# Low parts of raw operands by an adding DMA in the paired down projection of a two-layer encoder

## The chip, the cores and the metric

The kernel runs on one core of a Trainium2 chip. The metric is the time of one launch in microseconds of the device: the median of the runs before is 3236.0 us (three runs, 3235.75 to 3237.17).

## What is computed

Two post-norm layers of an encoder trunk over 1024 tokens of width 1024, float32 in and out. A layer has an input projection to four kinds of mixers, an output projection with a layer norm, a gated MLP with 2816 inner features and a layer norm, and a gated embedding with a layer norm. The change lies in the last product of the MLP:

```
f = silu(dwconv(h @ w_gate)) * (h @ w_up)      # [1024 tokens, 2816 features]
h = layer_norm(ALPHA * h + f @ w_down)         # w_down [2816, 1024]
```

## The kernel before

**Products in two parts.** TensorE multiplies tiles of a reduced float32 form (`F32R`). To keep the precision of float32, an operand is split in a high part, the value rounded to that form, and a low part, the rest. `split` (L92 to L94) does it in two operations: ScalarE copies the source to the high part (L84), and VectorE or GpSimd subtracts the high part from the source (L87). A product then is the sum of three: high with high, high with low, low with high (`p3`). The profile gives the helper's line for all such operations, L84 for ScalarE's and L87 for two-tile operations on VectorE or GpSimd; what they work on is told by the names of the tiles.

**The paired down projection** (`down_paired`, L1511 to L1621). Of the 22 tiles of 128 inner features, the first 20 go through it, in 5 rounds (`ch`) of 4 tiles. In a round the tokens fall in two halves, the outputs in two halves and the feature tiles in two pairs, so that the round is a product of 2 x 2 blocks, a11 to a22 (features) times b11 to b22 (weights). It is computed by Winograd's scheme with 7 products in place of 8. Each product has two operands, and each operand two tiles of 128 x 512 (the two feature tiles of a pair), to be split. Some operands are blocks as they come from memory (raw): a11 and b11 in product 1, a12 and b21 in product 2, b22 in product 3, a22 in product 4. The others are sums and differences of blocks (`comb`), made in place.

**Sources and tiles.** Features come from `fd` in DRAM, written by the stage before, into tiles named `fr`; weights come from `ffn_w_down` into tiles named `wr` (in round 0 two of the four into `wraw`). All are loaded by SyncE's queue in the order 0, 2, 1, 3. The split parts stand in tiles named `part`, one tile per operand with both parts; eight tiles share the tag, so four products' operands are alive at a time, and ScalarE's first pass of a new operand waits until TensorE is done with the one four products back. `part(srcs, eng)` (L1522) splits an operand; features' low parts are made on GpSimd, weights' on VectorE.

**The order of a round** is that of `operands` (L1555 to L1569): products 1, 2, 5, 7, 6, 3, 4, with the combinations between them, some on VectorE and some on GpSimd. Products are issued two operands behind (L1614 to L1621). Each product is four quarters of 128 tokens, six matmuls each (L1582). Product 1 of all rounds adds up in PSUM (`first`, tile `pp`). The other quarters are evicted: in round 0 products 5, 6, 7 by ScalarE to `E`, the others by VectorE to `H` with a factor (L90); in later rounds all by VectorE, added to `E` or `H` (L87). In the last round `merge` joins E and H.

**What sets the order on the engines.** Every engine works through its own queue in order. The queues are not written by hand: a planner that simulates the kernel with its own costs goes through the program, places instructions of neighbouring steps among one another, and puts in the waits. So the queues' order need not be that of the text, and where a step's operations change, the order around it can change too.

**Adding DMAs.** The kernel before has none. GpSimd's queue issues only DMAs that load the transform's constants and masks in the mixers (L397, L212 to L216); in the stage of the change all DMAs are SyncE's.

Of the kernel before, what the change touches and what calls it, by code (L numbers as in the profile page):

```python
# [28 lines left out]
# columns of the packed per-layer parameters  # L29
# [4 lines left out]
# feature tiles of the input projection  # L34
# [8 lines left out]
def interleave(*flows):  # L43
    """Emits flows, each (generator, number of its steps), in step with one another."""
    live = [[g, 0, n] for g, n in flows]
    while live:
        f = min(live, key=lambda f: f[1] / f[2])
        try:
            next(f[0])
            f[1] += 1  # L50
        except StopIteration:
            live.remove(f)


def stagger(items):
    """Emits the stages of items so that each item is one stage behind the one before it."""
# [18 lines left out]
class Trunk:  # L75
# [16 lines left out]
    def split(self, hi, lo, src, eng=None):  # L92
        self.act(hi, src)
        self.tt(lo, src, r(hi), ALU.subtract, eng)  # L94

# [50 lines left out]
    def to_x_after(self, x, H, t0, t1, ins, pair=False):  # L146
        """Transposes token tiles t0 to t1, once the products up to ins have freed the tiles that the
        result goes to."""
# [11 lines left out]
    def layer_norm(self, h, gb, eps=None, first=None):  # L160
        """The statistics; returns two functions that normalise h in place, one after the other."""
# [16 lines left out]
        def affine(c=512):  # L178
            """The first c columns, scaled already, on GpSimd, the others on VectorE."""
# [74 lines left out]
    def embed(self):  # L254
        """Normalises the input; the second half of the tokens only when the function that is returned runs."""
# [43 lines left out]
    def sin_of(self, fp, out, pre):  # L299
        """out = sin(pre) with the argument brought to [-pi, pi]."""  # L300
# [99 lines left out]
    def bruun(self, pool, zm, zp, C):  # L400
        """Residues of a polynomial of 1024 coefficients (8 blocks of 128 rows, C columns each)
        modulo the eight factors of x^2048 - 1 of degree 256; zm and zp are its residues modulo
        x^1024 - 1 and x^1024 + 1."""
# [36 lines left out]
    def conv_fft(self, l, n, pool, z, feature_major, out):  # L440
        """Circular convolution of z (token-major, 8 x 256) with filter n, and the skip term that the
        filter holds; the result is token-major [128, 8 * 256] or feature-major [128, 2, 8 * 128]."""
# [112 lines left out]
    def in_half(self, x, w, ps, hf):  # L555
        c0 = hf * 512
        if not isinstance(w, tuple):
            # the products of the high and the low parts of the weights, in separate rows
# [5 lines left out]
    def in_proj(self, l, x, tile_i):  # L564
        """One tile of 128 features, [128, 1024] in PSUM, in two steps."""
# [7 lines left out]
    def conv3(self, out, ps, cw):  # L573
        """Centred 3-tap convolution along the free dim with bias: cw columns w0, w1, w2, b."""
# [4 lines left out]
    def mixers(self, l, x, mu, late, st0):  # L579
# [9 lines left out]
        def scalars(su, ps):  # L589
            """Rotary key and dt, token-major."""  # L590
# [24 lines left out]
        def latent(pr, ti, k, rs, last, n):  # L615
            """A latent of attention with its gain, to DRAM; the sums of its squares go to rs."""
# [140 lines left out]
    def token_sums(self, sq):  # L757
        """Sums over features of the tiles sq [128 features, 512 tokens], as [128, 4] with tokens on partitions."""
# [5 lines left out]
    def squares(self, ss, g, hf, y, sq):  # L764
        """For the sums of squares of group g for 512 tokens, whose features are y, tokens on partitions:
        returns the function that finishes them on the tensor engine."""
# [6 lines left out]
    def ssd_scalars(self, l, mu, dtr):  # L773
# [5 lines left out]
        # softplus(x) = max(x, 0) + log1p(exp(-|x|)), the log by its series in e / (2 + e)  # L779
# [32 lines left out]
        # log(dt) - acs  # L812
# [6 lines left out]
    def ssd(self, l, ss, scal, xbc, zd, yd):  # L819
# [17 lines left out]
        def jv(a, c, g, n):  # L837
            """Columns (direction, head) of a group, broadcast over n."""
            return a[:, c, :].rearrange("p (d h) -> p d h", d=2)[:, :, 2 * g:2 * g + 2].unsqueeze(3).to_broadcast([128, 2, 2, n])

        def states(c, g):
            # token-major x and B, chunk states, forward scan
# [92 lines left out]
    def hl_products(self, out, terms):  # L935
        """Products of a [K, 2, 64] (hi and lo) with b, hi and lo: the sum of out[0:64] and out[64:128]."""
# [228 lines left out]
    def out_weights(self, l, g, pool):  # L1165
        """The rows of the output projection of a group, times the gains of its norm."""
# [12 lines left out]
    def out_proj(self, l, st, yd, ss, w, ahead):  # L1179
        nc, t = self.nc, self.t  # L1180
        hp = self.pool(st, f"hp{l}", 8, side=RIGHT)
        with ExitStack() as so:
# [17 lines left out]
            def scales(g):  # L1200
                # the residual branch is left unscaled: H holds the sum over ALPHA
# [73 lines left out]
    def blocks(self, todo, j):  # L1275
        """Transposes blocks of 128 tokens and 512 features, each (from, PSUM, (hi, lo)), to the
        128 tokens j of the operands."""
# [77 lines left out]
    def gate_up(self, l, H, hp, x, fd):  # L1355
        """The inner features of the MLP, to fd. Up and gate are the two rows of a product of blocks
        A (features x halves of D) and B (halves of D x halves of the tokens), by Winograd's scheme
        of seven products."""
        nc, t, pp = self.nc, self.t, self.pp[l]
        add, sub = ALU.add, ALU.subtract  # L1360
        with ExitStack() as st:
# [22 lines left out]
            def first(w1, w2, eng=None):  # L1384
                """The products of the first row of A and the first column of B."""
# [57 lines left out]
            for j in range(4):  # L1443
# [3 lines left out]
                # T1 = B12 - B11, T3 = B22 - B12, T2 = B22 - T1, and B21 - T2 for T4  # L1447
# [63 lines left out]
    def down_paired(self, l, fd, hmid, H, dp, ft):  # L1511
        """ALPHA times H plus the products of the first PAIRED inner features, by Winograd's scheme of seven
# [291 lines left out]
```

## Time and profile before

| | |
|---|---|
| median of three runs | 3236.0 us (3235.75 to 3237.17) |
| profiled execution, first to last instruction (its span) | 3236.6 us |
| mean granted TensorE clock, share of full speed | 0.965 |
| TensorE busy | 2976.9 us (92%) |
| VectorE busy | 2451.0 us (76%) |
| ScalarE busy | 1292.0 us (40%) |
| GpSimd busy | 1821.3 us (56%) |
| matmuls of the paired products (L1582), both layers | 1680 |

Only the span of the profiled execution is known, no time of its own beside it; it lies within the times of the runs. PE is TensorE, PEld its weight loads, DVE VectorE, ACT ScalarE, POOL GpSimd, SPq and POOLq the queues of DMA issues of SyncE and GpSimd. An instruction's row has its start and duration in us, engine, line, operation, the tile written and the tiles read, shapes, a count where several alike stand together, and in brackets the idle time of the engine before it with what ended it. Matmuls overlap, so a matmul's duration is longer than the distance to the next.

### The profile page before, as it was taken

The numbers are of one execution on the slowest core, as the hardware profiler recorded it, in microseconds if no ns is written. First come the engines' busy times: TensorE is split into PE (matmuls) and PEld (weight loads), VectorE is DVE, ScalarE is ACT, GpSimd is POOL, SyncE is SP. The second block draws the span as 40 slices with busy tenths as digits, with TensorE's granted clock in tenths as the row PEclk, the third lists the DMA queues.
The fourth block names the chain that finished last, engine by engine and source line by source line (L and its number), as shares of the span: only waits on it lengthen the run. The fifth ranks groups of instructions, "written<-read, shape, count | busy, mean of one in ns | idle before, by whom it ended". The sixth has DMA issues, their size and how long they took to land.

```text
span 3236.6 us, 40462 instructions
## 1 busy us (share of the span) xinstructions
PE 2976.9 (92%) x14316; PEld 2429.1 (75%) x14316; DVE 2451.0 (76%) x3711; ACT 1292.0 (40%) x2278; POOL 1821.3 (56%) x1371
## 2 busy tenths in 40 slices
PE   6999989998999999999989998899989999989996
PEld 4887866877777777777868877778777777767685
DVE  7678776878765557999777786778786555689986
ACT  4332365743333334333343323667333333343341
POOL 5455533527656556886435454345177555578855
PEclk9999998999999999999999998999999999999998
DMA  5566523022222225313335755130222222343232
GB/s 178 156 200 204 192 75 130 16 83 85 85 79 78 78 79 198 123 47 115 126 100 172 225 192 165 53 121 25 97 85 79 79 78 78 114 163 107 74 135 92
DMA packets 140468, 368.98 MB, mean 114 GB/s; under 512 B 15139, under 2 KB 42023, under 8 KB 140009
## 3 DMA queue, kind: packets, MB, share of 16 engines
q1 hardware_dynamic: 126008, 315.72, 28.8%
q0 software_dynamic: 14256, 50.67, 5.2%
q8 instruction: 114, 1.87, 0.2%
q14 instruction: 90, 0.73, 0.1%
HBM read 278.77 MB, written 87.56 MB: 113 GB/s over the span
## 4 chain that ended last, share of the span: by engine, by line
PE 39%; DVE 21%; POOL 16%; issue 10%; DMA 10%; ACT 4%; SPq 0%; POOLq 0%; DVEq 0%; ACTq 0%
PE ps L99 18%; PE pp L99 13%; POOL w L87 5%; DMA wraw<-in_ffn_w_gate_dram 4%; POOL wraw L87 4%; DVE part L87 3%; POOL u L87 2%; DVE fr L87 2%; POOL H L87 2%; PE ps L942 2%; DVE H L90 2%; DVE s L87 1%; POOL part L87 1%; DVE H L87 1%; DMA wraw<-in_ffn_w_up_dram 1%
## 5 line engine op out<-in xcount | busy, mean ns | idle before, releaser
L99 PE MATMUL ps<-x,w 128*128 128x512 f32 x2112 | 508.2, 394 | 11.3 <-ACT v L84 6.1
L99 PEld LDWEIGHTS ps<-x,w 128*128 128x128 f32 x2112 | 400.1, 190 | 99.1 <-ACT v L84 7.0
L99 PE MATMUL pp<-x,wh 128*128 128x512 f32 x1344 | 427.9, 397 | 1.8 <-ACT wh L84 1.8
L99 PE MATMUL ps<-xq,w 128*128 128x512 f32 x1584 | 391.1, 397 | 29.7 <-DVE u L87 24.3
L1582 PE MATMUL ps<-part 128*128 128x512 f32 x1440 | 351.2, 399 | 33.8 <-DVE H L87 10.8
L99 PEld LDWEIGHTS ps<-xq,w 128*128 128x128 f32 x1584 | 292.9, 188 | 117.2 <-DVE u L87 50.7
L1582 PEld LDWEIGHTS ps<-part 128*128 128x128 f32 x1440 | 270.9, 191 | 110.5 <-DVE H L87 20.3
L99 PEld LDWEIGHTS pp<-x,wh 128*128 128x128 f32 x1344 | 254.9, 192 | 54.3 <-ACT wh L84 2.0
L87 POOL TENSOR_TENSOR w<-wraw,w 128x512 fp32r<-128x512 f32 x164 | 217.5, 1345 | 116.0 <-ACT w L84 116.0
L99 PE MATMUL pp<-x,wl 128*128 128x512 f32 x672 | 266.5, 397 | 3.8 <-POOL wl L87 3.8
L84 ACT ACTIVATE w<-wraw 128x512 fp32r<-128x512 f32 x264 | 151.8, 622 | 268.0 <-DMA wraw<-in_ffn_w_up_dram 218.6
L87 POOL TENSOR_TENSOR wl<-wraw,wh 128x1024 fp32r<-128x1024 f32 (+2 forms) x61 | 152.8, 2507 | 182.7 <-ACT wh L84 124.2
L87 POOL TENSOR_TENSOR part<-fr,part 128x512 fp32r<-128x512 f32 x120 | 192.4, 1628 | 47.2 <-ACT part L84 42.2
L87 DVE TENSOR_TENSOR s<-wraw 128x512 f32<-128x512 f32 x44 | 55.4, 1259 | 202.2 <-DMA wraw<-in_ffn_w_gate_dram 199.8
L99 PE MATMUL ps<-wo,yn 128*128 128x512 f32 x768 | 189.7, 405 | 5.4 <-DVE H L90 3.0
L1039 POOL TENSOR_TENSOR P<-P,smr 128x1024 f32<-128x1024 f32 x64 | 121.1, 1893 | 112.2 <-DVE smr L1038 103.3
L99 PEld LDWEIGHTS ps<-wo,yn 128*128 128x128 f32 x768 | 147.1, 195 | 39.4 <-DVE H L90 4.8
L90 DVE SCALAR_TENSOR_TENSOR g<-g,pp 128x1023 f32<-128x1023 f32 x88 | 126.6, 1439 | 57.7 <-ACT g L84 57.7
L87 POOL TENSOR_TENSOR u<-u,g 128x512 f32<-128x512 f32 x44 | 78.7, 1788 | 152.5 <-ACT g L84 152.3
L87 DVE TENSOR_TENSOR part<-wr,part 128x512 fp32r<-128x512 f32 x124 | 158.2, 1299 | 4.8 <-ACT part L84 4.8
L99 PE MATMUL ps<-wh,x 128*128 128x512 f32 x512 | 158.8, 391 | 0.0
L99 PEld LDWEIGHTS pp<-x,wl 128*128 128x128 f32 x672 | 128.5, 191 | 30.5 <-POOL wl L87 4.7
(381 smaller groups left out, 7038.7 us busy)
## 6 DMA issues: line engine op xcount, KB each, us to landing
c_fwd<-in_c_fwd_dram POOLq DMA_DIRECT2D x64, 512.0 KB, 5.1
wraw<-in_ffn_w_up_dram SPq DMA_DIRECT2D x50, 512.0 KB, 3.5
wraw<-in_ffn_w_gate_dram SPq DMA_DIRECT2D x44, 512.0 KB, 4.5
f<-u SPq DMA_DIRECT2D x88, 256.0 KB, 2.0
wraw<-in_w_in_dram SPq DMA_DIRECT2D x42, 512.0 KB, 4.1
fr<-f SPq DMA_DIRECT2D x40, 512.0 KB, 4.5
wr<-in_ffn_w_down_dram SPq DMA_DIRECT2D x36, 512.0 KB, 6.4
c_inv<-in_c_inv_dram POOLq DMA_DIRECT2D x32, 512.0 KB, 5.0
```

The costliest lines, as they stand in the source:

```text
L84: self.nc.scalar.activation(out, in_, func, **kw)
L87: (eng or self.nc.vector).tensor_tensor(out, a, b, op=op)
L90: return self.nc.vector.scalar_tensor_tensor(out, a, s, b, op0=op0, op1=op1)
L99: ins = self.nc.tensor.matmul(out, a, b, start=i == 0, stop=i == n - 1)
L942: ins = self.nc.tensor.matmul(out[0:64] if j else out, v[:, 0, :] if j else v.rearrange("p i d -> p (i d)"), terms[i][1 + j], start=k == 0 ...
L1039: nc.gpsimd.tensor_tensor(P, P, sm.to_broadcast([128, T]), op=ALU.mult)
L1582: nc.tensor.matmul(ps, u, v, start=k == 0 and (p != 1 or ch == 0), stop=k == 5 and (p != 1 or ch == last))
```

## The change

The low parts of the raw operands are no longer subtracted by VectorE or GpSimd. ScalarE writes the high part as before, and then, from the same source, its negative into the place of the low part, rounded to the same form. A DMA issued by GpSimd's queue then reads the same block once more from DRAM (`fd` or `ffn_w_down`) and adds it to what stands there, which leaves source minus high part. In rounds 1 to 4 this is done for all six raw operands; in round 0 the two of product 1 are split as before, so four are changed. The operands made by combinations are split as before. The rest of the diff removes comments and docstrings only.

```diff
+    def split_added(self, hi, lo, src, far):
+        self.act(hi, src)
+        self.act(lo, src, scale=-1.0)
+        self.nc.gpsimd.dma_start(lo, far, accum_op=ALU.add)
...
-        def part(srcs, eng):
+        def part(srcs, eng, far=None):
             hl = self.xp.tile([128, 2, 2, 512], F32R, name="part", tag="X")
             for i, v in enumerate(srcs):
-                self.split(hl[:, i, 0], hl[:, i, 1], v, eng)
+                if far is None:
+                    self.split(hl[:, i, 0], hl[:, i, 1], v, eng)
+                else:
+                    self.split_added(hl[:, i, 0], hl[:, i, 1], v, far[i])
             return hl
...
-            F, W = {}, {}
+            F, W, fF, fW = {}, {}, {}, {}
             for k in (0, 2, 1, 3):
                 f = 4 * ch + k
+                fF[k], fW[k] = fd[f], t["ffn_w_down"][l, f * 128:(f + 1) * 128, :]
...
+            p11, p12, _, p22 = ([fF[2 * i + k][:, h] for i in range(2)] for h in (h0, h1) for k in range(2))
+            q11, q21, _, q22 = ([fW[2 * i + k][:, h] for i in range(2)] for h in (h0, h1) for k in range(2))
...
-            def operand(p, a, b):
-                return p, part(a, nc.gpsimd), part(b, nc.vector)
+            def operand(p, a, b, fa=None, fb=None):
+                return p, part(a, nc.gpsimd, fa), part(b, nc.vector, fb)
 
-            yield operand(1, a11, b11)
-            yield operand(2, a12, b21)
+            yield operand(1, a11, b11, p11 if ch else None, q11 if ch else None)
+            yield operand(2, a12, b21, p12, q21)
...
-            yield operand(3, a12, b22)
+            yield operand(3, a12, b22, None, q22)
             comb(b21, b11, b21, sub, nc.gpsimd)
-            yield operand(4, a22, b21)
+            yield operand(4, a22, b21, p22)
```

## Rows read from the trace of the kernel before

**Rows 1.** The page's head: span, and busy us of each engine.
```profile
span 3236.6 us, 40462 instructions
...
PE 2976.9 (92%) x14316; PEld 2429.1 (75%) x14316; DVE 2451.0 (76%) x3711; ACT 1292.0 (40%) x2278; POOL 1821.3 (56%) x1371
```

**Rows 2.** Stretches: length, busy us (instructions) per engine, clock, DMA share, GB/s.
```profile
1260.00:1280.00 20.00, 15.12 (x55) 10.85 (x53) 20.00 (x18) 10.26 (x19) 17.74 (x11) 0.91 0.32 93
1300.00:1320.00 20.00, 14.23 (x54) 10.53 (x53) 20.00 (x18) 7.25 (x14) 20.00 (x13) 0.91 0.03 8
1340.00:1360.00 20.00, 19.72 (x86) 15.69 (x85) 19.32 (x21) 8.12 (x16) 18.68 (x13) 1.00 0.04 6
2900.00:2920.00 20.00, 14.94 (x57) 11.17 (x56) 20.00 (x22) 7.89 (x15) 18.30 (x12) 0.91 0.31 106
```

**Rows 3.** Line 1582: what ended its engine's idle time (us, times).
```profile
  DVE H L87: 31.0, 37
  DVE part L87: 22.7, 14
  DVE E L87: 13.4, 21
  ACT E L84: 13.3, 12
  DVE H L90: 12.1, 9
```

**Rows 4.** Timeline of TensorE at both ends of the stage, both layers.
```profile
1251.77 5.60 PE L1582 MATMUL pp<-part 128*128 128x512 f32 x24
1257.21 3.11 PE L1582 MATMUL ps<-part 128*128 128x512 f32 x13
...
1467.50 4.82 PE L1582 MATMUL ps<-part 128*128 128x512 f32 x18 [0.54 <-DVE H L87]
...
2845.68 5.60 PE L1582 MATMUL pp<-part 128*128 128x512 f32 x24
...
3060.28 4.83 PE L1582 MATMUL ps<-part 128*128 128x512 f32 x18 [0.59 <-DVE H L87]
```

**Rows 5.** The splits: the page's groups, then ScalarE's copies with min/median/max in ns.
```profile
L87 POOL TENSOR_TENSOR part<-fr,part 128x512 fp32r<-128x512 f32 x120 | 192.4, 1628 | 47.2 <-ACT part L84 42.2
L87 DVE TENSOR_TENSOR part<-wr,part 128x512 fp32r<-128x512 f32 x124 | 158.2, 1299 | 4.8 <-ACT part L84 4.8
...
L84 ACT ACTIVATE part<-fr x120: 613/625/637, 1235.3 to 3041.0; 128x512 fp32r<-128x512 f32 x120
```

**Rows 6.** Timeline of VectorE and GpSimd, side by side and VectorE alone.
```profile
1300.52 1.74 POOL L87 TENSOR_TENSOR part<-tg,part 128x512 fp32r<-128x512 f32 x1
1301.03 1.78 DVE L87 TENSOR_TENSOR tg<-fr 128x512 f32<-128x512 f32 x1
...
1334.52 0.68 DVE L87 TENSOR_TENSOR fr<-tg,fr 128x512 f32<-128x512 f32 x1
```

**Rows 7.** Timeline of GpSimd: two DMA issues, one after the other.
```profile
222.88 1.10 POOL L397 DMA_DIRECT2D c_fwd<-in_c_fwd_dram  x2
```

**Rows 8.** DMA: GpSimd's queue, a 256 KB store, landing of the 512 KB loads from GpSimd.
```profile
q0 software_dynamic: 14256, 50.67, 5.2%
...
f<-u SPq DMA_DIRECT2D x88, 256.0 KB, 2.0
...
DMA to landing us min/median/max: 3.7/5.1/8.1
```

**Rows 9.** Timeline of round 0 in layer 0, ahead of its second product.
```profile
1253.62 3.98 POOL L87 TENSOR_TENSOR wraw<-wr,wraw 128x512 f32<-128x512 f32 x2
...
1255.27 1.19 DVE L87 TENSOR_TENSOR part<-wr,part 128x512 fp32r<-128x512 f32 x1
```

**Rows 10.** Timeline of the start of round 2 in layer 0.
```profile
1330.29 1.16 ACT L84 ACTIVATE part<-fr 128x512 fp32r<-128x512 f32 x2 [3.23 <-issue]
...
1335.48 0.62 PE L1582 MATMUL pp<-part 128*128 128x512 f32 x2
```

## The prediction

> **What bounds the kernel now.** The page comes first: TensorE is busy for 92% of 3236.6 us and VectorE for 76% [rows 1], so over the whole span TensorE seems to be the limit. That is an average, and the change touches one stage of each layer, the paired down projection, so the second view is the table of stretches there [rows 2]. In a good stretch (1340 to 1360) TensorE starts 86 matmuls in 20 us. In 1260 to 1280 and 1300 to 1320 it starts 55 and 54, and layer 1 has its like (57 in 2900 to 2920). In all four VectorE is busy for 19.3 to 20.0 of the 20 us and GpSimd for 17.7 to 20.0. VectorE and GpSimd are full in the good stretch too, so TensorE lives on what they have done ahead, and loses where their work bunches.
>
> How much is lost follows from the pace. The first product of a round takes 24 matmuls and the next begins 5.44 us after it, which is 0.227 us for each [rows 4]. The stage has 5 rounds of 7 products of 24 matmuls, 840 in a layer, so 190.4 us if TensorE never waits. It runs from 1251.8 to 1472.3 in layer 0 and from 2845.7 to 3065.1 in layer 1 [rows 4]: 220.5 and 219.4 us. About 30 us of a layer, 59 us in all, is lost; nothing done to this stage's operands can give back more.
>
> What the loss waits for is the third view, the idle time of the engine ahead of these matmuls [rows 3]. It counts matmul and weight load together, so its sum is larger than 59 us and I use it for shares only. VectorE ends 31.0 + 22.7 + 13.4 + 12.1 = 79.2 of it, ScalarE's evictions 13.3: some 83% is VectorE, mostly the evictions of products (H, E) that stand in its queue behind splits and combinations.
>
> Why VectorE is late is seen in single instructions [rows 6]. A combination of two SBUF tiles took 0.68 us at 1334.5, with GpSimd idle, and 1.78 us at 1301.0, beside a GpSimd subtraction of 1.74 us. The two engines slow one another, so taking operations from both counts for more than the operations themselves.
>
> **The change, part by part.** *Removed.* A raw operand is two tiles, so 6 raw operands are 12 splits a round; round 0 has 4 raw operands with 8. That is 4 x 12 + 8 = 56 a layer, 112 in all, half of them on each engine. VectorE loses 56 x 1.299 = 72.7 us, GpSimd 56 x 1.628 = 91.2 us [rows 5]; per full round 7.8 and 9.8 us.
>
> *Added on ScalarE.* 112 passes that write the negated high part, 0.62 us each [rows 5], 69 us in all or 7.4 us a full round. ScalarE is busy for 7.3 to 10.3 of 20 us in the stretches [rows 2], so a round of some 44 us has over 20 us free: cost nothing, hidden by the engine's own idle time. Without that cover it would be the whole 69 us. In round 0 it also stands ahead of ScalarE's own evictions (E), so I allow one pass, 0.6 us a layer.
>
> *Added on GpSimd.* 112 issues. The nearest row is the transform's constants, two issues in 1.10 us [rows 7], 0.55 us each: 62 us in all against 91 removed, 6.6 against 9.8 a round. GpSimd gains 3 us a round. An adding DMA is not in the trace: the lower end is nothing, if GpSimd passes it on at once, the upper one 1.6 us, as long as the subtraction. At 0.81 us each GpSimd gains nothing. I take 0.55, the only issue from GpSimd that the trace shows. GpSimd's queue is in order: an issue that waits for ScalarE's negated part holds back the combinations of b11 and b12 behind it, and through them VectorE's and ScalarE's splits of products 5 and 7. The removed subtraction waited at the same place, for the pass one earlier.
>
> *Added in the DMA engines.* 112 x 256 KB = 29.4 MB. The GpSimd queue moved 50.67 MB in 5.2% of the span [rows 8], so 256 KB is 0.87 us of all engines, 10.4 us for twelve; a round also loads eight tiles of 512 KB, 13.9 us by the same rate. If the addition doubles it, 20.9 + 13.9 = 35 us, still under the 44 us of a round. Landing takes between 2.0 us (a 256 KB store) and 8.1 us (the longest 512 KB load from GpSimd); I take that load's median, 5.1 us [rows 8].
>
> The Trainium skill has a rule against the change: "Collectives: The Full Stack", section "The bandwidth ceiling: the fold count and why AG ≠ RS ≠ AR", says that a DMA that adds reads two sources and that this halves the rate it measured. No run here shows it. By it the doubled figure above would hold, and the stage would still not be bound by its transfers.
>
> *Latency.* A matmul now waits for ScalarE's second pass, the issue and the landing. At the start of round 2 ScalarE begins the first operand at 1330.3 and its matmuls begin at 1335.5 [rows 10], 5.2 us. The new way takes four passes, 2.5 us, 0.55 and 5.1: 8.1 us, so 3 us late. The product before it has 24 matmuls, 5.4 us, to fill in, and four operands are alive at once, so for rounds 1 to 4 I take no cost (bounds 0 and 6 us a round, the latter with landings of 8.1 us). Round 0 has no such cover: its second operand's low part began on VectorE at 1255.3 and was used at 1257.2 [rows 4, 9]; GpSimd is then in two combinations of 4.0 us until 1257.6, behind which an issue may stand. Landing would be at about 1261: 4 us late, bounds 0 and 7.
>
> *What comes back, per layer.* Round 0, stretch 1260 to 1280: 20 - 55 x 0.227 = 7.5 us lost; four splits of VectorE go, 5.2 us, half of them where VectorE is not late: 2.6 (0 to 5.2). Start of round 1, stretch 1300 to 1320: 7.8 us lost; the four splits of its first two products go: 5.2 (0 to 7.8). The other 15 us of the 30 lie in small pieces; the merge at the end and ScalarE's evictions, some 3 us, stay, and of the 12 left I take half, 6 (0 to 12), because the queue order is written anew and something else will be late next: VectorE and GpSimd slowing one another as in [rows 6], and TensorE itself. Together 13.8, less 4 and 0.6: 9.2 us a layer, 18.4 in all.
>
> The profiled execution's span is 3236.6 us, 0.6 above the median of the runs, 3236.0, so nothing measurable lies around the span. 3236.6 - 18.4 = 3218.2, and against the median 3217.6.
>
> **The rivals.** *A: the full return.* TensorE becomes the bound through the stage: 25 us of each layer's 30 return, round 0's delay falling where VectorE was late anyway. For it: VectorE at 20.0 of 20, and the double effect in [rows 6]. Against: the merge and ScalarE's evictions stay. 3236 - 50 = 3186.
>
> *B: no measurable change.* The adding DMA costs GpSimd 0.8 us or more to issue, so that GpSimd is as full as now (20.0 in one stretch of [rows 2]) and its combinations are late instead of VectorE's evictions; the 5.2 us at round 1's start return and 4 to 5 are paid in round 0. 3236, within 6.5. For it: GpSimd's 17.7 to 20.0. Against: 0.55 us for a plain issue. That the low parts never leave the engines is excluded by the diff.
>
> *C: slower, by the landing.* Beside the eight loads of a round, an adding DMA lands after 8 us and not 5. Its place is the first operands of each round: past 7.6 us (5.1 and the 2.5 us that are left of the 5.4 us of cover) TensorE stands. At 11 us, which is the 8.1 us of [rows 8] and the 3 us that a queue of loads may add, each of rounds 1 to 4 loses 3.4 us on the first operand and as much on the second, 27 us a layer, and round 0 loses 7: 34 against 13.8 returned, 2 x 20 = 40 us, 3276. It decides from about 8.4 us on, where 8 x (8.4 - 7.6) + 7 equals those 13.8. Against it: the median of 5.1 us is for twice the bytes.
>
> *D: slower, by the rate.* If the addition itself runs at a third of the copy rate, 2.6 us for 256 KB, twelve take 31 us beside 13.9 of loads, 45 us: a round of 44 us is then bound by its transfers. It decides from 2.5 us on, (44 - 13.9) / 12. At 3.1 us a round takes 51.1 us, 7.1 more, which over 56 / 12 rounds and two layers is 66 us: 3302.
>
> **How the numbers follow.** The forecast, faster by 7 to 36 us, has 0.50; A 0.07; B 0.17; C 0.16; D 0.10. About 0.2% of the time, 6.5 us, is what a measurement of this kernel can tell from no change. Faster: 0.50 + 0.07 = 0.57. Within: 0.17. Slower: 0.26. The predicted time is the forecast's, 3217.6. The likeliest case's own range is 3200 to 3229. For 8 in 10 the range reaches down to A's 3186 and up to 3255, which takes in B and the milder half of C and leaves out the rest of C, D and a little under A: about 0.2.
>
> **What would show it.** Right: in 1300 to 1320 and its like TensorE starts over 65 matmuls where it started 54; VectorE's busy time falls by more than 73 us, because its remaining operations get shorter too, and the mean of its remaining splits is below 1.30 us; GpSimd's issues are near 0.55 us; the stage lasts about 211 us a layer. Wrong: matmuls that wait for a DMA onto "part" by more than 10 us in all (C), issues over 0.8 us (B), a DMA busy share over 0.9 through whole rounds (D). If VectorE is no longer full and TensorE still starts 54 matmuls there, my reading that VectorE's queue made it wait was wrong; if it is late in round 0 by much more than 4 us, the cover that I gave rounds 1 to 4 is doubtful as well.

## The result, and the profile after

The changed kernel takes 3285.0 us against 3236.6 for the kernel before, measured side by side: a ratio of 1.0152 (95% interval 1.0139 to 1.0165), 49 us slower. A second measurement gave 1.0160 (1.0132 to 1.0188). The forecast was 3217.6 us in a range of 3186 to 3255.

The page after: its head, the queue that GpSimd feeds (q0), and the round's own loads of features and weights, whose last number is the median time to landing. It answers to [rows 1, 8]; the two loads took 4.5 and 6.4 us to land before.

```profile
span 3283.2 us, 40748 instructions
...
PE 2992.7 (91%) x14316; PEld 2445.0 (74%) x14316; DVE 2405.9 (73%) x3655; ACT 1350.9 (41%) x2390; POOL 1802.4 (55%) x1427
...
q0 software_dynamic: 30384, 80.03, 10.3%
...
fr<-f SPq DMA_DIRECT2D x40, 512.0 KB, 6.9
wr<-in_ffn_w_down_dram SPq DMA_DIRECT2D x36, 512.0 KB, 10.9
```

VectorE is less busy than before by 45.1 us, and GpSimd by 18.9, and yet the program is longer. TensorE's timeline at both ends of the stage, both layers, answers to [rows 4]:

```profile
1251.67 5.60 PE L1594 MATMUL pp<-part 128*128 128x512 f32 x24
...
1493.02 1.65 PE L1594 MATMUL ps<-part 128*128 128x512 f32 x6 [0.86 <-DVE H L87]
...
2868.38 5.60 PE L1594 MATMUL pp<-part 128*128 128x512 f32 x24
...
3109.60 1.65 PE L1594 MATMUL ps<-part 128*128 128x512 f32 x6 [0.85 <-DVE H L87]
```

The stage lasts 243.0 and 242.9 us where it lasted 220.5 and 219.4. That is 46.0 us more, and the spans differ by 46.6: the whole loss is in this stage. The stretches of layer 0 [rows 2], with the whole stage of both layers as the last two rows:

```profile
1260.00:1280.00 20.00, 14.08 (x44) 10.37 (x44) 17.41 (x17) 9.46 (x17) 15.41 (x10) 0.83 0.49 126
1300.00:1320.00 20.00, 12.82 (x43) 9.64 (x43) 19.27 (x14) 10.00 (x19) 16.66 (x15) 0.83 0.80 208
1340.00:1360.00 20.00, 16.63 (x66) 12.95 (x65) 18.39 (x22) 9.44 (x18) 15.89 (x15) 0.91 0.95 219
1380.00:1400.00 20.00, 13.18 (x47) 10.12 (x46) 17.21 (x18) 8.66 (x17) 12.81 (x13) 0.78 1.06 240
1252.00:1495.00 243.00, 209.78 (x842) 166.57 (x840) 189.65 (x206) 117.29 (x210) 173.70 (x141) 0.92 0.64 158
2868.00:3111.00 243.00, 207.61 (x843) 165.07 (x841) 187.76 (x205) 116.89 (x210) 173.24 (x141) 0.92 0.64 158
```

Read the third column pair and the last three numbers. VectorE does 206 operations in the stage where it did 233, so it should be far from full, but in 1300 to 1320 it is busy for 19.27 us with 14 operations: they are long. The DMA share stands at 0.80 to 1.06 where rounds 1 to 3 start. TensorE idles, the mean granted clock of these stretches is 0.78 to 0.91, between its two levels (0.5 is 1.2 GHz, 1.0 is 2.4 GHz), and the same 840 matmuls take 209.8 us where they took 200.9 (the stage of before is shown further down). So some 9 of the 22.5 us that layer 0 lost are longer busy time of the same matmuls, beside a clock of 0.92 in the stage against 0.98 before; the rest is idle time.

What ended TensorE's idle time ahead of these matmuls, for [rows 3]:

```profile
  DVE E L87: 72.9, 24
  DVE H L90: 33.0, 15
  ACT E L84: 16.8, 8
  DMA part<-in_ffn_w_down_dram: 11.3, 6
  DVE part L87: 6.6, 4
  DVE H L87: 6.3, 8
```

The waits for VectorE's splits fell from 22.7 to 6.6 us, as the change intends. The waits for its evictions rose: E from 13.4 to 72.9, and E and H (both lines) together from 56.5 to 112.2. The adding transfers themselves end 11.3 us. The groups on VectorE and GpSimd [rows 5, 7] and the adding transfer's landing:

```profile
L87 DVE TENSOR_TENSOR part<-wr,part 128x512 fp32r<-128x512 f32 x68 | 86.1, 1300 | 19.3 <-ACT part L84 19.3
L87 DVE TENSOR_TENSOR tg<-fr 128x512 f32<-128x512 f32 x20 | 27.5, 1380 | 34.9 <-DMA fr<-f 34.9
...
L87 POOL TENSOR_TENSOR part<-fr,part 128x512 fp32r<-128x512 f32 x64 | 96.6, 1532 | 22.7 <-ACT part L84 22.7
L100 POOL DMA_DIRECT2D part<-in_ffn_w_down_dram x56 | 66.5, 1286 | 19.6 <-ACT part L84 19.1 <-issue 0.3
L100 POOL DMA_DIRECT2D part<-f x56 | 54.3, 1087 | 63.7 <-ACT part L84 30.5 <-DMA wr<-in_ffn_w_down_dram 16.4 <-PE ps L1594 14.5
...
DMA to landing us min/median/max: 3.9/7.2/13.6
```

The splits that are left on GpSimd are a little shorter (1532 ns, before 1628), those on VectorE are not (1300, before 1299). An adding issue holds GpSimd for 1.29 and 1.09 us, not 0.55. VectorE's first combination of a round (tg) waits 34.9 us for its features; before it was 6.8. The timeline at the start of round 3 of layer 0 shows what a late eviction looks like:

```profile
1386.29 1.27 POOL L100 DMA_DIRECT2D part<-in_ffn_w_down_dram  x1
1386.71 6.20 DVE L87 TENSOR_TENSOR tg<-fr 128x512 f32<-128x512 f32 x1 [0.17 <-DMA fr<-f]
1386.85 2.02 POOL L87 TENSOR_TENSOR wr<-wr 128x512 f32<-128x512 f32 x1
1388.09 1.63 POOL L100 DMA_DIRECT2D part<-in_ffn_w_down_dram  x1
...
1388.70 3.54 POOL L87 TENSOR_TENSOR wr<-wr 128x512 f32<-128x512 f32 x2
1391.15 2.85 POOL L100 DMA_DIRECT2D part<-f  x2
1392.30 3.39 POOL L87 TENSOR_TENSOR wr<-wr 128x512 f32<-128x512 f32 x1
...
1394.50 0.68 DVE L87 TENSOR_TENSOR E<-E,ps 128x512 f32<-128x512 f32 x1
...
1395.23 8.59 PE L1594 MATMUL ps<-part 128*128 128x512 f32 x24 [6.37 <-DVE E L87]
```

One combination on VectorE takes 6.20 us, while GpSimd alternates issues and combinations. It took 0.68 alone and 1.78 beside one GpSimd operation [rows 6]. Below, an operation that is stretched in this way is called held. The evictions E stand behind it, and TensorE waits 6.37 us for the first. This is the picture to test: is it the issues, the bytes, or the landing that costs?

### The profile page after: what moved, and what is told of

Read it like the earlier page. It is cut to its first block, busy times and chain, and to the rows that moved or that the text cites. A ratio compares the mean times of both kernels' runs of the same rounds, so it can differ in the third digit from the quotient of the medians.

```text
span 3283.2 us, 40748 instructions
## 1 busy us (share of the span) xinstructions
PE 2992.7 (91%) x14316; PEld 2445.0 (74%) x14316; DVE 2405.9 (73%) x3655; ACT 1350.9 (41%) x2390; POOL 1802.4 (55%) x1427
## 3 DMA queue, kind: packets, MB, share of 16 engines
q0 software_dynamic: 30384, 80.03, 10.3%
## 5 line engine op out<-in xcount | busy, mean ns | idle before, releaser
L105 PE MATMUL ps<-x,w 128*128 128x512 f32 x2112 | 508.2, 393 | 11.8 <-ACT v L84 6.2
L1594 PE MATMUL ps<-part 128*128 128x512 f32 x1440 | 361.4, 409 | 68.6 <-DVE E L87 33.8
L1594 PEld LDWEIGHTS ps<-part 128*128 128x128 f32 x1440 | 282.9, 198 | 143.0 <-DVE E L87 39.0
L105 PE MATMUL ps<-wo,yn 128*128 128x512 f32 x768 | 190.5, 406 | 5.8 <-DVE H L90 3.0
L84 ACT ACTIVATE part<-fr 128x512 fp32r<-128x512 f32 x176 | 99.4, 624 | 177.5 <-issue 93.7
L87 DVE TENSOR_TENSOR w<-wraw,w 128x512 fp32r<-128x512 f32 x100 | 124.1, 1246 | 12.5 <-ACT w L84 12.2
```

Of the source, the lines that this page charges most:

```text
L84: self.nc.scalar.activation(out, in_, func, **kw)
L87: (eng or self.nc.vector).tensor_tensor(out, a, b, op=op)
L105: ins = self.nc.tensor.matmul(out, a, b, start=i == 0, stop=i == n - 1)
L1594: nc.tensor.matmul(ps, u, v, start=k == 0 and (p != 1 or ch == 0), stop=k == 5 and (p != 1 or ch == last))
```

## The experiments

Every kernel was measured beside the kernel before on the same chip. So that they can be added, the table gives each ratio as microseconds of 3236.6 (ratio less 1, times 3236.6); an interval is about 5 us to either side. "Stage" is the length in layer 0 and 1, "VectorE" its busy time in the stage (mean of the layers), "longest" the longest VectorE operation on two SBUF tiles among combinations and splits, "features" the combinations' wait for features in both layers, all from the profiled run. That is one execution of each, and what lies outside the two stages scatters by some us from kernel to kernel; the stages' lengths leave that out.

| kernel | us against before | ratio, 95% interval | stage | VectorE | longest | features |
|---|---|---|---|---|---|---|
| before | 0 | | 220.5, 219.4 | 211.6 | 1.8 | 6.8 |
| no_dma | -21 | 0.9935 (0.9921 to 0.9950) | 207.0, 206.7 | 169.1 | 2.5 | 8.7 |
| sp_bytes | -15 | 0.9954 (0.9940 to 0.9967) | 208.3, 209.3 | 169.5 | 2.4 | 9.0 |
| sp_bytes2 | -3 | 0.9992 (0.9980 to 1.0005) | 210.6, 218.2 | 166.8 | 1.8 | 26.6 |
| tiny_copy | -7 | 0.9977 (0.9961 to 0.9994) | 211.2, 209.8 | 176.6 | 6.1 | 10.7 |
| tiny | +7 | 1.0021 (1.0005 to 1.0036) | 211.5, 222.4 | 190.5 | 6.0 | 8.4 |
| late_ops | +14 | 1.0043 (1.0029 to 1.0056) | 221.3, 222.9 | 189.6 | 1.8 | 34.0 |
| copy_junk | +15 | 1.0047 (1.0030 to 1.0063) | 222.1, 221.9 | 184.8 | 6.0 | 4.0 |
| copy | +21 | 1.0065 (1.0047 to 1.0083) | 226.0, 223.0 | 181.7 | 5.3 | 19.6 |
| half | +43 | 1.0132 (1.0111 to 1.0152) | 235.8, 241.3 | 192.4 | 6.4 | 21.0 |
| add_junk | +45 | 1.0140 (1.0125 to 1.0155) | 232.9, 237.7 | 194.9 | 8.7 | 11.8 |
| after | +49 | 1.0152 (1.0139 to 1.0165) | 243.0, 242.9 | 188.7 | 6.2 | 34.9 |
| merged | +54 | 1.0168 (1.0149 to 1.0187) | 248.6, 240.4 | 189.5 | 7.5 | 25.3 |

The theories: **I**, the issues cost (GpSimd's time, and VectorE beside them); **B**, the bytes and additions in the DMA engines cost; **L**, the matmuls wait for the landing; **O**, the order of the work, written anew, costs. The planner writes the queues anew for almost every edit: compared instruction by instruction, only copy has the order of the change in every queue, and only tiny and tiny_copy have the same order as one another. Any other step from kernel to kernel holds a change of order too.

**no_dma** takes the transfer away and keeps all else.

```diff
-        self.nc.gpsimd.dma_start(lo, far, accum_op=ALU.add)
```

> The changed kernel without its adding DMAs: the 112 low parts stay the negated high parts (so the low parts' share of those products is wrong). Three theories for the 48 us that the change costs. I (issues): GpSimd's DMA issues, in turn with its two-tile operations, keep VectorE's two-tile operations from starting, so that VectorE's evictions are late. B (bytes): the adding DMAs fill the DMA engines at the start of each round, so that the loads of features and weights land late and VectorE's combinations wait for them. O (order): the planner's new order of the queues is what costs. By I and B everything comes back and the removed subtractions pay: 3205 to 3230 us. By O (the order is written anew here as well, but with the same passes) it stays above 3255.

Measured 3209.5 us, 21 us faster than before, and 26.2 us shorter in the two stages. The removal of 112 splits less ScalarE's second passes is worth about what was forecast (26.4); the passes by themselves were not measured. The whole loss, some 70 us from here to the change, comes with the adding transfers (and the order that they bring). The stage's row, of before and then of this kernel (columns as in [rows 2]):

```profile
1252.00:1472.00 220.00, 200.89 (x840) 157.50 (x839) 212.83 (x233) 88.48 (x155) 183.91 (x114) 0.98 0.31 105
```

```profile
1251.00:1458.00 207.00, 197.49 (x842) 159.98 (x840) 170.60 (x205) 116.14 (x209) 131.41 (x86) 0.98 0.33 115
```

VectorE loses 42 us of its 213, the other operations get shorter too, and the granted clock stays at 0.98.

**tiny** and **tiny_copy** issue as often but move 16 bytes of each row; the second does not add.

```diff
-        self.nc.gpsimd.dma_start(lo, far, accum_op=ALU.add)
+        self.nc.gpsimd.dma_start(lo[:, 0:4], far[:, 0:4], accum_op=ALU.add)   # tiny
+        self.nc.gpsimd.dma_start(lo[:, 0:4], far[:, 0:4])                     # tiny_copy
```

> Every adding DMA adds only the first 4 of 512 columns (the rest of each low part stays the negated high part): the same number of issues and of rows, 1/128 of the bytes. Theory B: the loads land as before, 3205 to 3235 us. Theory I: VectorE's two-tile operations of 3 to 6 us stay, 3260 to 3290. Both in equal parts: about 3250.

> As in the kernel that adds 4 columns, but the DMAs copy those 4 columns instead of adding them (the rest of each low part stays the negated high part); the order of all queues is the same. So far: without DMAs 22 us faster than before, 112 adding issues without bytes 28 us more than that, the bytes another 43. If an issue costs by the time that it takes on GpSimd (0.55 us here, 0.9 to 1.2 when adding), half of the 28 us comes back: 3218 to 3228. If it costs by standing between GpSimd's two-tile operations at all: 3232 to 3240.

Measured 3237.4 and 3226.2 us; the first lies between what the theories gave. With hardly a byte, the plain issues cost 14 us over no_dma and the adding ones 28. The stage of layer 0 in tiny:

```profile
1252.00:1464.00 212.00, 198.11 (x843) 159.05 (x842) 189.64 (x206) 116.33 (x209) 175.88 (x141) 0.98 0.39 112
```

Against no_dma the same 205 operations of VectorE take 19 us more, and GpSimd's row grows by 44 us, its 55 issues among it. The table's column "longest" shows why: without issues from GpSimd in the stage (before, no_dma, the SyncE runs) no two-tile operation takes over 2.5 us, and in late_ops, whose issues stand where no combination runs (24 of the 40 run beside a split on VectorE), none over 1.8. In every other kernel with issues the longest takes 5.3 to 8.7. So theory I holds for a part: 28 of 70 us, of which the 14 from plain to adding issues are measured at one order.

Not every held operation has an issue beside it. The longest split on VectorE in tiny (4790 ns in the row of min/median/max) begins at 1306.35; GpSimd meanwhile goes through four operations without an issue:

```profile
L87 DVE TENSOR_TENSOR part<-wr,part x68: 677/1178/4790, 1284.3 to 3036.6; 128x512 fp32r<-128x512 f32 x68
...
1305.32 2.77 POOL L87 TENSOR_TENSOR wr<-wr 128x512 f32<-128x512 f32 x2
1307.83 2.75 POOL L87 TENSOR_TENSOR part<-fr,part 128x512 fp32r<-128x512 f32 x2
```

That the issues bring about the held operations is what the comparison of kernels shows; how they do it is open.

**copy** moves all bytes without adding; the queues' order is the change's, instruction by instruction.

```diff
-        self.nc.gpsimd.dma_start(lo, far, accum_op=ALU.add)
+        self.nc.gpsimd.dma_start(lo, far)
```

> Every adding DMA becomes a plain copy of the same block over the low part (which then holds the whole value): the order of all queues is the same as in the changed kernel, the bytes read from HBM too, but nothing is added. Theory B: a 256 KB DMA takes about 0.9 us of the engines and not 1.5, loads land sooner, 3255 to 3270 us. Theories I and O: 3280 to 3290, unless an issue becomes shorter than its 0.9 to 1.2 us.

Measured 3252.0 us, a little below theory B's range: 28 us faster than the change (by the ratios; 33 between the medians) at the same order. So the order cannot be the whole loss, and 28 us are the price of adding, with its longer issue, engine time and landing together. An effect of order within the 42 us from no_dma to copy is not excluded. Against tiny_copy the bytes cost 28 us, against tiny the full addition costs 42 in the change, at another order each.

**late_ops** leaves the adding transfers on products 3 and 4 alone, 40 of 112; products 1 and 2 have their splits back.

```diff
-            yield operand(1, a11, b11, p11 if ch else None, q11 if ch else None)
-            yield operand(2, a12, b21, p12, q21)
+            yield operand(1, a11, b11)
+            yield operand(2, a12, b21)
```

> The adding DMA for b22 and a22 alone (products 3 and 4, all rounds; 40 DMAs in place of 112); the four operands of products 1 and 2 are split as before the change. Theories I and B: about 40/112 of the cost or less, since products 1 and 2 stand where the loads of a round land: 3235 to 3255 us. If what costs is the latency at the start of a round alone: 3225 to 3236. Theory O gives no number.

Measured 3245.9 us, +14, where 40 of 112 of the change's loss would be +17. No operation is held here (longest 1.8), but the features are late by 34.0 us in all, as in the change: 32 of the 40 transfers are under way beside the round's loads. Only 4 us of the loss lie in the stages of the profiled run (444.2 against 439.9 us), which was also the slowest of six, 3255.9.

**merged** has one transfer for the two tiles of an operand, 56 of 512 KB.

```diff
-                    self.split_added(hl[:, i, 0], hl[:, i, 1], v, far[i])
+                    self.split_added(hl[:, i, 0], hl[:, i, 1], v, far)
+            if far is not None:
+                self.nc.gpsimd.dma_start(hl[:, :, 1], far, accum_op=ALU.add)
...
```

> The changed kernel with one adding DMA per operand, for both of its tiles: 56 issues of 512 KB in place of 112 of 256 KB, the same result. If an issue costs by itself, some 14 of the 28 us come back: 3265 to 3273. If it costs by its rows (256 in place of 128), nothing: 3278 to 3290. The low part of the first tile lands later, with that of the second, which can take some of it back.

Measured 3287.2 us: nothing came back. GpSimd's issues fell from 121 us to 81, but VectorE's operations were held as long (7.5), and TensorE waited 34.2 us for the transfers, which landed after 7.8, where it had waited 11.3. So fewer issues did not help, but the later landing can have hidden what they gave.

**after_fr6**, **before_fr6**, **after_fr6b**, **before_fr6b** give the features two more buffers, so that they can be loaded earlier; in the pair "b" only from round 1 on.

```diff
-            for k in (0, 2, 1, 3):
+            for k in (1, 3, 0, 2) if ch else (0, 2, 1, 3):
...
-                F[k] = self.wp.tile([128, T], F32, name="fr", tag="whl", bufs=4)
+                F[k] = self.wp.tile([128, T], F32, name="fr", tag="whl", bufs=4) if k % 2 or ch == 0 else dp.tile([128, T], F32, name="fr", tag="FR", bufs=2)
```

> The changed kernel with two more buffers for the feature tiles of the rounds (6 in place of 4), and the tiles 1 and 3 loaded first, so that the loads of a round start about two products sooner. If the bytes cost because the features land late and VectorE's combinations wait for them with the evictions behind them, 20 to 35 of the 43 us come back: 3250 to 3265. If they cost by the landing of the adding DMAs themselves: 3275 to 3290.

> The same two buffers and the same order of loads in the kernel before, as the control: features are waited for there for some 2 to 5 us a layer, so 3226 to 3237.

> The last pair of kernels had a fault: the two new buffers lie in a pool that opens only when the stage before is done, and round 0's first product waited some 15 us for them in both. Here round 0 uses the old buffers; from round 1 on tiles 0 and 2 have the new ones. If the bytes cost because the features land late, the changed kernel costs 15 to 30 us more than its control here, not 48 to 53. If they do not, the difference stays 45 to 55.

> The control for it: the kernel before, with the same two buffers and the same order of loads. 3226 to 3240 us.

Measured 3317.5 and 3284.9 us, then 3307.6 and 3257.0. Both controls and the first changed kernel missed what was expected; the second pair's difference is the second of its two cases. The first pair is spoilt: round 0's first product waited 15.3 to 15.5 us a layer for its operand, whose buffers stand in a pool that opens only after the stage before; the difference within it is 33 us. In the second pair the control, too, is 0.8% slower than before, and in both kernels round 0's second product waits for ScalarE (12.5 us with the change, 10.6 without), so the edit is not neutral. The difference that the change makes stays at 50.5 us there. The combinations' wait for features fell from 34.9 to 18.8 us, and TensorE's for the adding transfers rose from 11.3 to 66.2: the lateness moved from one wait to the other. Nothing was recovered there; which pair is the better test is open.

**after_again** repeats the change, and **sp_bytes** and **sp_bytes2** move the same blocks by SyncE, once or twice, into tiles that nobody reads.

```diff
-        self.nc.gpsimd.dma_start(lo, far, accum_op=ALU.add)
+        self.nc.sync.dma_start(self.junk.tile([128, 512], F32, name="junk", tag="junk", bufs=4), far)
...
```

> The changed kernel once more, on the same chip as its variants: 3280 to 3290 us.

> No DMA from GpSimd: the same 112 blocks of 256 KB are loaded by SyncE's queue into a tile that nobody reads (the low parts stay the negated high parts). So the bytes without GpSimd's issues. If the bytes cost by themselves, as the copying kernel less the one that copies 4 columns suggests (some 20 us): 3222 to 3235 us. If all of it came with GpSimd's issues: 3206 to 3214, as without DMAs. SyncE's own queue gets 112 entries more, which can add to either.

> No adding transfers (the low parts stay the negated high parts); SyncE loads each of the 112 blocks of 256 KB twice into unread tiles, 58.7 MB, at 0.87 us of engines each 1.74 us a pair, more engine time than the 1.52 us that an adding transfer took. The blocks loaded once took 3216.1 us against 3209.5 without any. If busy DMA engines as such make the round late (share), this should lose as the adding transfers do without gating: above 3250 us. If it is the GpSimd queue's way of moving them that costs (its issue, and VectorE and GpSimd beside it), this stays at 3218 to 3232 us, with VectorE's busy time in the stage at about 170 us.

Measured 3286.3, 3216.1 (between the two ranges) and 3232.9 us. The same bytes by SyncE cost 6 us over no_dma, where the intervals overlap, twice the bytes 18. The stage of layer 0 in sp_bytes2:

```profile
1256.00:1466.00 210.00, 198.31 (x840) 159.54 (x838) 167.76 (x205) 115.18 (x208) 130.62 (x86) 0.98 0.72 251
```

The DMA engines are busier (0.72) than in the change (0.64), and TensorE keeps its clock (0.98, and 0.96 in layer 1). So busy DMA engines as such are not what costs 49 us. Still the features are late by 26.6 us in all, and 18 us are lost with no operation held. A rival cause was not tested: the loads stand in one queue with these transfers, and that queue waited 71.0 us for features, and 66.7 for weights, to land in an unread tile before its next transfer.

**copy_junk** and **add_junk** keep issue, queue and bytes, and let nobody wait for the landing.

```diff
-        self.nc.gpsimd.dma_start(lo, far, accum_op=ALU.add)
+        self.nc.gpsimd.dma_start(self.junk.tile([128, 512], F32, name="junk", tag="junk", bufs=4), far)   # copy_junk
+        self.nc.gpsimd.dma_start(self.junk[0], far, accum_op=ALU.add)                                     # add_junk
+        self.junk.append(self.junk.pop(0))
...
```

> The same 112 transfers of 256 KB are issued by GpSimd as plain loads into tiles that nobody reads, and the low parts stay the negated high parts, so no matmul waits for any of them. The plain copy onto the low parts took 3252.0 us, the copy of four columns of each 3226.2, the kernel without transfers 3209.5. If the bytes cost because TensorE's operands are only complete when they have landed (gating), this run keeps the issues and the bytes but not the waiting: 3222 to 3232 us. If they cost because they crowd the round's loads and the features land later (crowding), it stays near the copy: 3244 to 3256 us, and VectorE's combinations wait for the features for about 10 us a layer as in the copy.

> The same 112 adding transfers of 256 KB go onto four tiles a layer that are zeroed once and never read (in turn, so that each waits for the one four before it); the low parts stay the negated high parts. The whole change took 3286 us, the adding transfers of four columns 3237.4. If gating by the landing is what the full bytes cost, this is 3233 to 3243 us. If the crowding of the round's loads is, it stays at 3275 to 3295 us, with the combinations' waits for the features at 16 to 19 us a layer. Something between would divide the cost between the two.

Measured 3245.7 and 3275.2 us, 6 below copy and 4 below the change (6 by its second ratio); both pairs of intervals overlap. The stages are 5 and 15 us shorter. So theory L is worth between 4 and 15 us, not clear of noise, and with a change of order in it (copy_junk's transfers also move in 80 packets each, copy's in 144). The half of the crowding theory that named the features was missed: copy_junk's combinations wait 4.0 us for them, not some 20, and add_junk's 11.8, not over 32. What stays in copy_junk is held operations, as its combinations show (min/median/max in ns):

```profile
L87 DVE TENSOR_TENSOR fr<-fr x40: 676/688/5507, 1264.6 to 3036.0; 128x512 f32<-128x512 f32 x40
L87 DVE TENSOR_TENSOR tg<-fr x20: 675/686/2732, 1262.8 to 3031.8; 128x512 f32<-128x512 f32 x20
L87 DVE TENSOR_TENSOR fr<-tg,fr x20: 676/1380/5050, 1272.4 to 3034.8; 128x512 f32<-128x512 f32 x20
```

In add_junk GpSimd's issues rose to 1.85 us on the mean and some waited for the tile used four before (8 us), so it is a little harsher than the change in that respect.

**half** adds 256 of the 512 columns.

```diff
-        self.nc.gpsimd.dma_start(lo, far, accum_op=ALU.add)
+        self.nc.gpsimd.dma_start(lo[:, 0:256], far[:, 0:256], accum_op=ALU.add)
```

> The adding transfers of the change with 256 of the 512 columns each (half the bytes, as many issues; the other half of each low part stays the negated high part). Four columns took 3237.4 us, all 512 took 3286. If the cost grows with the bytes: 3256 to 3268 us. If it has a point from which the transfers of a round no longer fit beside its loads: 3237 to 3248 us, or, if that point lies below half the bytes, 3275 us and more.

Measured 3277.7 us: 36 more than four columns, and 7 less than all of them (the intervals overlap, and the order differs from either). No growth with the bytes can be told from here on. The queue's share in half is 8.1%, that of the plain copy, and the transfers land after 4.7 us on the median; TensorE waits for them 0.3 us in all. Neither landing nor engine time can then be what puts it 22 us above copy. Its timeline at the start of round 1:

```profile
1298.00 2.14 POOL L100 DMA_DIRECT2D part<-f  x2
...
1299.15 2.31 POOL L87 TENSOR_TENSOR wr<-wr 128x512 f32<-128x512 f32 x1
1299.47 5.18 DVE L87 TENSOR_TENSOR fr<-fr 128x512 f32<-128x512 f32 x1
1300.39 1.92 POOL L100 DMA_DIRECT2D part<-in_ffn_w_down_dram  x1
...
1304.57 1.87 DVE L90 SCALAR_TENSOR_TENSOR H<-H,ps 128x512 f32<-128x512 f32 x3
1305.30 2.85 PE L1594 MATMUL ps<-part 128*128 128x512 f32 x8 [3.77 <-DVE H L90]
```

And the same place in tiny:

```profile
1297.10 5.20 DVE L87 TENSOR_TENSOR fr<-fr 128x512 f32<-128x512 f32 x1
...
1302.23 1.87 DVE L90 SCALAR_TENSOR_TENSOR H<-H,ps 128x512 f32<-128x512 f32 x3
1302.96 1.89 PE L1594 MATMUL ps<-part 128*128 128x512 f32 x7 [1.83 <-DVE H L90]
```

The held operation is as long (5.18 and 5.20 us) and the same evictions stand behind it. In half it begins 2.4 us later, TensorE's own work ahead of it only 0.4 us later (1297.29 against 1296.88), and the wait is 3.77 us instead of 1.83. VectorE has no slack there, so what makes it late adds to the hold; this is read from one place in two kernels.

**Where the 70 us went, and what stays open.** From no_dma to the change, by the ratios: 14 us for 112 issues by GpSimd, 14 more for their adding form, some 38 for bytes that nobody waits for (tiny to add_junk), 4 for the landing. By the stages' lengths these steps are 7, 13, 37 and 15 of 72 us. Only the second is between kernels of one order; the others hold an effect of order that no run measures.

How the bytes cost is shown only in part. VectorE is as busy in tiny as in the change (190.5 and 188.7 us a stage), so the full bytes add no further hold: the 52 us by which the change's two stages are longer are waiting, half of it for features (34.9 us against 8.4). In copy_junk it is the other way: against no_dma its stages are 30 us longer, VectorE is busy for 31 us more, and the features are not later. Late features alone (sp_bytes2, longest operation 1.8 us) cost 18 us over no_dma; plain issues and bytes with no late features (copy_junk) cost 36; the change has both at once. This is an account of one engine's time. That the two together make up the loss is argued from it, not shown by a run. More buffers for the features did not bring it back, and why half of the bytes cost nearly as much as all is open. No version found here keeps the adding transfer and beats the kernel before.

## Why the prediction was wrong

**The return was right.** The forecast without the transfer's own latency was 13.8 less 0.6 a layer, 26.4 us; in no_dma the stages, 207.0 and 206.7 us, are 26.2 us shorter, and the time 21 (16 to 26). VectorE's queue was what TensorE waited for. The sum rests in part on halves taken by guess (2.6 of 5.2, 6 of 12), so that it came out this near may be partly luck.

**Round 0 was right.** Its second product was to be 4 us late; the timeline after has TensorE waiting 2.6 us for that transfer, and a little before it:

```profile
1261.06 5.30 PE L1594 MATMUL ps<-part 128*128 128x512 f32 x15 [2.58 <-DMA part<-in_ffn_w_down_dram]
```

**The latency of rounds 1 to 4, taken as nothing, was nearly right.** The landing rose to 7.2 us on the median, not 5.1, still under the 8.4 from which rival C decided; L is worth 4 to 15 us, round 0 included. C named a time close to the measured one, by a mechanism that did not cause it: its sign, waits on a DMA onto "part" over 10 us, came out at 11.3, and the stage lost 46.

**The issue was the first step that failed.** I took 0.55 us from [rows 7], two plain issues one after the other; the adding form takes 1.29 and 1.09. Rival B had the right price (above 0.8) and nearly the right answer for this term alone: tiny, with those issues and almost no bytes, is at +7 us where B said 0 with 6.5 to either side. But GpSimd did not stay full, as B had it (16.66 of 20 us in 1300 to 1320, 20.00 before); the price is not only paid by GpSimd. I counted [rows 6] in one direction, that fewer operations make the others shorter. With the issues put between GpSimd's combinations, single VectorE operations are up to 6.2 us long in the change and up to 8.7 in add_junk, which no row of before could show, since its paired stage has no issue from GpSimd in it. VectorE's busy time fell by 45 us, not by more than 73.

**The bytes were the second, and by the runs the larger.** They were taken to cost nothing because 35 us are "still under the 44 us of a round", which treats a round as one pool of time; tiny to the change is 42 us. The addition ran at 1.52 us of the engines for 256 KB (q0's share of 10.3% less 5.2% of the span before, 170 us over 112 transfers), below the doubled 1.74, so the sum was even a little too high. But the transfers bunch at the starts of rounds, where the share is 0.80 to 1.06 against 0.64 on the mean, together with the loads that VectorE's first combination needs. Rival D looked at the round as a whole too, and its point of 2.5 us was not reached.

The factor there is 1.75 over the 0.87 us of [rows 8], and 1.8 over the 0.84 us of the copy kernel (8.1% in its page). The rule that I weighed (the Trainium skill, "Collectives: The Full Stack", section "The bandwidth ceiling: the fold count and why AG ≠ RS ≠ AR": an add reads two sources, so half the rate) points the right way; here the measured 1.8 decides, and it was not this term that failed.

**The signs.** Of those named as right none came: 43 matmuls in 1300 to 1320 instead of over 65, splits of 1300 ns on VectorE instead of under, 243 us instead of 211 for the stage. Of those named as wrong three came at least in part: issues over 0.8 us, a DMA share over 0.9 (at the starts of rounds, not through whole rounds), and 11.3 us of waits on a DMA onto "part". The last one, that my reading of VectorE's queue would be wrong, did not: TensorE waits for VectorE more than ever, for evictions behind held operations.

## What to carry to other kernels

A DMA that does an engine's arithmetic is not free of the engines: price its issue in the form that will be used (here 1.1 to 1.3 us against 0.55 for a plain one), and look at who runs beside the issuing engine, since VectorE operations on two SBUF tiles were held for up to 8.7 us in the kernels with issues between GpSimd's operations. Compare a transfer with the time at the place where it runs, not with the mean of a round, and ask which load the next engine needs first there. A run with four columns of each transfer, and one into a tile that nobody reads, divide issue, bytes and waiting for little effort. Compare the order of the queues before such runs are subtracted: here it was the same in two pairs only.

## What the runs showed of the hardware

- An adding issue from GpSimd takes 1.09 to 1.29 us on the mean in the change, a plain one of the same shape 0.55 to 0.56; with four columns instead of 512 these are 1.24 to 1.55 and 0.55 to 0.56. The issue's length does not come from the bytes.
- While GpSimd alternates issues and operations on two tiles, a VectorE operation on two SBUF tiles can last 6.2 us, across two issues and three GpSimd operations; an eviction with one input in PSUM takes 0.68 us soon after it, while GpSimd is still in a combination (the E row above). The Trainium skill ("SBUF — State Buffer", section "Who interferes with whom") says that a VectorE instruction with two SBUF inputs contends with a GpSimd instruction that reads SBUF, and that one with at most one SBUF input does not, outside the 2-port perf modes. The traces agree on both. That a hold outlasts a single GpSimd operation is measured here, with issues between (6.2 against 1.78 us) and, in tiny, also over four operations without one (4.79 us); why, no run shows.
- 29.4 MB loaded by SyncE into the same stages cost 6 us, issued by GpSimd 36 us over the same kernel without them (sp_bytes and copy_junk against no_dma; the queues' orders differ, and the 6 us are not clear of noise).
